# The first MLP product of a hybrid attention block in seven block products, and another order for the last output rows

## The chip, the cores and the metric

The kernel runs on one core of a Trainium2 chip. The metric is the time on the device in microseconds (us), as the median over runs. TensorE (PE, with its weight loads PEld) multiplies matrices, VectorE (DVE), ScalarE (ACT) and GpSimd (POOL) work elementwise, SyncE (SP) issues transfers. POOL and ACT can issue transfers as well. Each engine takes its own instructions in order and waits for the others on semaphores.

## The reference, cut to what matters

```python
h = x                                   # 512 rows x 1024
n = rmsnorm(h, g_mix); proj = n @ w_in  # two attention branches from here
h = h + merged @ w_out                  # merged: both branches, gated
m = rmsnorm(h, g_mlp)
h = h + jnp.square(jax.nn.relu(m @ w_ff1)) @ w_ff2    # w_ff1 1024 x 4096, w_ff2 4096 x 1024
return rmsnorm(h, g_final)
```

All in float32. The change lies in the first quarter of `m @ w_ff1` and in the last `rmsnorm`.

## The kernel before, in words

Every float32 matrix is split into a high part, rounded by ScalarE, and a low part, the difference, made by VectorE. A product is three matmuls (`mm3`, lines 88 to 90): high by high, and the two mixed ones. The two passes that make the parts are called the split of an operand; for a weight tile of 128 x 2 x 512 (1024 elements a partition) they are line 1616 (`hi`) and line 1620 (`lo`).

The MLP runs in four quarters of the 4096 hidden columns. In each quarter a first product (`f`, m by a 1024 x 1024 part of w_ff1) is followed by a second (`g`, its activated result by the matching part of w_ff2). Both factors are cut into 2 x 2 blocks. All the groups but the first, f0, use seven block products instead of eight: sums of the left blocks, sums of the right (weight) blocks, and sums of the results. For the left factor these sums are `m_sum` (line 1519, VectorE), split by `m_hi` and `m_lo` (lines 1508 and 1512); they are made once and serve all quarters. For the right factor `sum` adds blocks in place, by VectorE (line 1628) in the `f` groups and by a transfer issued by POOL that adds to what lies in the tile (line 1626) in the `g` groups. Each block product has 16 chunks (two column halves b, two row tiles i, four parts p of the contraction), each of three matmuls of 128 x 256: 48 matmuls. Weight block x lies in two tiles g (parts 0 and 1, and parts 2 and 3 of the contraction), and there are four such pairs: `wq` for B11, B12, B21 and `ring` for B22. `sink` takes a finished accumulator to where it goes: for f groups into the blocks `f..a..`, then relu, square, sums and splits for the second product.

f0 alone is `plain`: eight block products with the four weight blocks each used twice, B12, B11, B21 and B22 split two times, no weight sums. It starts right after the output projection (`wo_product`), while the residual rows 2 and 3 are still being finished: `add_rows` (line 1465) adds a finished part of the projection to the rows, `first_half_square` and `second_half_square` (line 174) give the sums of squares, `row_rstd` (VectorE line 181, POOL line 184) the reciprocal root, line 1847 the scaled rows, `flipped` (line 198) transposes them on TensorE, `m_copy` (ACT line 1503 or VectorE line 1501) takes the transposed blocks out of PSUM. Rows 0 and 1 come first and give column half 0 of m (blocks 1 and 2 of `m_raw`); rows 2 and 3 are transposed between the first and second block product and give blocks 4 and 0.

The order is written by hand: `step(at, what, ...)` puts each piece at a place on a line of time (100 units stand for about 1 us of TensorE), the steps are sorted by place, and `in_program_order` fixes that order on PE, ACT and DVE. For the quarters, `PLACES` holds the places; f0 has its own, `F0_RIGHT`. SP's and POOL's transfers are not in that fixed order: a scheduler places them, each behind the work that it has to wait for.

The last rows: for rows 0 and 1 the steps `out_first` (square of the right half, and the product of rows and final gain on POOL, line 1718), `out_square`, `out_left` (line 1729), `out_store`; for rows 2 and 3, `last_rows` runs the last block product in three pieces (one for rows 2, two halves for rows 3), adds them (line 1749), and then squares (line 1722), root (lines 1725, 181, 184), scaling (lines 1729, 1733) and store.

## Time and profile before

| what | value |
|---|---|
| median of 3 runs (lowest, highest) | 744.96 us (744.7, 745.11) |
| the profiled execution, and its span | 745.58 us, 743.9 us |
| TensorE busy, mean granted clock | 732.8 us, 0.995 |
| VectorE, ScalarE, GpSimd busy | 627.1, 493.3, 209.7 us |
| f0's first matmul, the second product's first | 412.09, 460.57 us |
| TensorE's last matmul, last store issued | 734.33, 739.89 us |

Times inside a run count from the start of the span. A timeline row has start, duration, engine, source line, operation, output tile, input tiles, shape, and in brackets how long the engine was idle before and what ended that. The duration of a row overlaps the next instruction on the engine by some 0.1 us, so the pitch (start to start) is what a queue costs. Buffer numbers are left out of tile names: `f030h` is f0, product 3, half 0, high part; `mh` and `ml` are the parts of m's blocks, `mb` the transposed banks, `w` and `w220f`, `w221f` the weight tiles, `h` the residual rows, `hp` their sums and roots, `ms` their scratch and output. A row of a stretch has its start and end, its length, busy time and count of PE, PEld, DVE, ACT and POOL, the granted clock, the busy share of the DMA engines and GB/s.

### The profile page before, as it was taken

The page shows a single profiled execution, that of the slowest core. Times are in us where ns is not written, and L with a number is a line of the kernel's source. Part 1 is how long each engine was busy: PE and PEld are TensorE (multiplying, and loading weights), DVE is VectorE, ACT ScalarE, POOL GpSimd, SP SyncE. Part 2 cuts the span into 40 slices and gives each one's busy share as a digit, 9 for nine tenths or more (in the row PEclk, how much of TensorE's full clock was granted, in tenths as well). Part 3 has the DMA queues.
Part 4 walks back from the last instruction along what each step waited for, and adds up shares of the span by engine and source line. Part 5 has one row for each costly group of instructions (what it writes and reads, how often), then busy time and mean ns, then how long its engine had stood idle before and what let it go on. Part 6 is the DMA issues. An engine that isn't in the chain of part 4 may idle for free.

```text
span 743.9 us, 11549 instructions
## 1 busy us (share of the span) xinstructions
PE 732.8 (99%) x4274; PEld 648.4 (87%) x4274; DVE 627.1 (84%) x863; ACT 493.3 (66%) x803; POOL 209.7 (28%) x276
## 2 busy tenths in 40 slices
PE   9999999999999999999999999999999999999995
PEld 7888888888888888898988999889988998899984
DVE  7777887889998787898898778998699869987896
ACT  7556575686596675888856778545774477537764
POOL 0732020242754633146751011100211012101215
PEclk9999999999999999999999999999999999999998
DMA  9849682521221334459887048761987087816763
GB/s 305 276 108 225 205 176 86 92 52 28 74 56 43 50 82 113 108 118 235 247 184 209 32 124 216 176 165 57 242 185 197 9 246 175 195 56 150 166 111 113
DMA packets 78344, 105.76 MB, mean 142 GB/s; under 512 B 15792, under 2 KB 34224, under 8 KB 78288
## 3 DMA queue, kind: packets, MB, share of 16 engines
q1 hardware_dynamic: 63088, 75.64, 32.8%
q0 software_dynamic: 14912, 29.10, 23.2%
q8 instruction: 33, 0.54, 0.3%
q10 hardware_dynamic: 288, 0.28, 0.1%
q14 instruction: 23, 0.19, 0.1%
HBM read 100.03 MB, written 2.10 MB: 137 GB/s over the span
## 4 chain that ended last, share of the span: by engine, by line
PE 93%; DVE 3%; issue 1%; ACT 1%; DMA 1%; POOL 0%; POOLq 0%; DVEq 0%; ACTq 0%
PE first L326 3%; PE tp L1122 2%; PE zb L88 1%; PE zb L89 1%; PE zb L90 1%; PE f3x L89 1%; PE f2x L90 1%; PE f3x L90 1%; PE f1x L90 1%; PE f1x L89 1%; PE f2x L89 1%; PE f2x L88 1%; PE f1x L88 1%; PE f3x L88 1%; PE av L89 1%; PE av L88 1%
## 5 line engine op out<-in xcount | busy, mean ns | idle before, releaser
L1626 POOL DMA_DIRECT2D w<-in_w_ff x32 | 38.6, 1205 | 262.3 <-DMA w<-in_w_ff 148.6
L1102 DVE TENSOR_REDUCE top<-s 128x1 f32<-128x512 f32 x32 | 21.6, 681 | 4.8 <-PE s L90 4.7
L1107 ACT ACTIVATE e<-s,top 128x512 f32<-128x512 f32 x32 | 22.0, 688 | 3.5 <-DVE top L1102 2.5
L94 DVE TENSOR_TENSOR pT<-tp,pT 128x512 fp32r<-128x512 f32 x32 | 21.8, 682 | 2.4 <-ACT pT L93 1.9
L93 ACT ACTIVATE pT<-tp 128x512 fp32r<-128x512 f32 x32 | 19.1, 596 | 3.2 <-PE tp L1122 3.2
L1122 PE MATMUL tp<-ident,e 128*128 128x128 f32 x128 | 19.4, 274 | 0.0
L88 PE MATMUL av<-pT,v 128*128 128x256 f32 x64 | 19.1, 299 | 0.0
L90 PE MATMUL av<-pT,v 128*128 128x256 f32 x64 | 18.2, 285 | 0.0
L89 PE MATMUL av<-pT,v 128*128 128x256 f32 x64 | 18.1, 283 | 0.0
L1122 PEld LDWEIGHTS tp<-ident,e 128*128 128x128 f32 x128 | 15.2, 140 | 3.2 <-ACT e L1113 0.7
L94 POOL TENSOR_TENSOR qF<-qk,qF 128x512 fp32r<-128x512 f32 x4 | 6.6, 1643 | 37.5 <-ACT qF L93 37.5
L667 POOL DMA_DIRECT2D gvw<-in_w_in x4 | 4.9, 1232 | 38.7 <-DVE gvw L672 34.0
L1628 DVE TENSOR_TENSOR w<-w,w 128x1024 f32<-128x1024 f32 x12 | 14.4, 1221 | 0.1
L667 POOL DMA_DIRECT2D zaw<-in_w_in x4 | 4.9, 1228 | 32.7 <-DVE zaw L672 28.0
L88 PE MATMUL s<-kbuf,q 96*128 96x512 f32 x32 | 14.1, 439 | 0.0
L980 POOL DMA_DIRECT2D w<-in_w_out x10 | 12.2, 1399 | 6.5 <-DVE bo60l L94 5.3
L1153 POOL TENSOR_TENSOR mx<-tb,yg 128x256 f32<-128x256 f32 x8 | 7.7, 964 | 19.7 <-DVE tb L1150 13.8
L577 ACT ACTIVATE bds<-bd 128x512 f32<-128x512 f32 x4 | 2.4, 598 | 15.8 <-PE bd L555 15.8
L89 PE MATMUL s<-kbuf,q 96*128 96x512 f32 x32 | 12.6, 395 | 0.0
L90 PE MATMUL s<-kbuf,q 96*128 96x512 f32 x32 | 12.6, 393 | 0.0
L1113 ACT ACTIVATE e<-e,tot 128x512 f32<-128x512 f32 x16 | 11.6, 726 | 1.3 <-DVE tot L1112 1.3
L89 PEld LDWEIGHTS av<-pT,v 128*128 128x128 f32 x64 | 12.2, 190 | 0.3
(2167 smaller groups left out, 3269.2 us busy)
## 6 DMA issues: line engine op xcount, KB each, us to landing
w<-in_w_ff SPq DMA_DIRECT2D x48, 512.0 KB, 5.2
w<-in_w_ff POOLq DMA_DIRECT2D x32, 512.0 KB, 6.3
w<-in_w_out POOLq DMA_DIRECT2D x10, 512.0 KB, 9.0
grw<-in_w_in SPq DMA_DIRECT2D x8, 512.0 KB, 8.5
zaw<-in_w_in SPq DMA_DIRECT2D x8, 512.0 KB, 7.2
gvw<-in_w_in SPq DMA_DIRECT2D x8, 512.0 KB, 4.6
w<-in_w_out SPq DMA_DIRECT2D x16, 256.0 KB, 5.7
w220f<-in_w_ff SPq DMA_DIRECT2D x8, 512.0 KB, 5.0
```

What stands on the lines that cost most here:

```text
L88: nc.tensor.matmul(acc, lh, rh, start=start, stop=False, skip_group_check=onto)
L89: nc.tensor.matmul(acc, lh, rl, start=False, stop=False, skip_group_check=onto)
L90: nc.tensor.matmul(acc, ll, rh, start=False, stop=stop, skip_group_check=onto)
L93: nc.scalar.activation(hi, src, AF.Copy)
L94: rest.tensor_tensor(lo, src, raw(hi), op=ALU.subtract)
L326: nc.tensor.matmul(f_accs[i], a[:, i * P : (i + 1) * P], b, start=k == 0 and x == 0, stop=k == KD - 1 and x == 2)
L980: nc.gpsimd.dma_start(d, rows.rearrange("(k t p) w -> p t k w", t=2, p=P)[:, x // 2], accum_op=ALU.add)
L1102: nc.vector.tensor_reduce(top, acc, axis=AX.X, op=ALU.max, negate=True)
L1107: nc.scalar.activation(e, acc, AF.Exp, bias=top, accum_out=tot[:, qt % 2 : qt % 2 + 1])
L1122: nc.tensor.transpose(tp[:, k * P : (k + 1) * P], e[:, k * P : (k + 1) * P], ident)
L1626: nc.gpsimd.dma_start(d, self.source(src, g), accum_op=ALU.add)
L1628: nc.vector.tensor_tensor(d, d, self.tiles(src)[g], op=ALU.add)
```

## The change

f0 takes the seven-product form of the other f groups, in the order 1, 2, 5, 6, 7, 4, 3, so `PLAIN` and its branches go. Its weight sums are made by adding transfers on POOL, as in the g groups: `sum(3)` adds B22 to the tile of B12 before f0 starts, `sum(1)` adds B12, `sum(2)` B22 and `sum(4)` B21 to the tile of B11, each after the split that uses the tile's content until then. The left block sums are needed one product after the transposes, so `m_sum` puts blocks 5 and 6 into tiles of their own, all eight copies are ScalarE's, and the places of f0's steps are new. The accumulators of product 5 and 3 lie in the other PSUM pool, and product 5's weight parts in another pool of tiles. f0's hidden blocks go through the same `relu`, `square` and sums as in the other quarters. The places of all later work start 386 units earlier (`FLIPS` 190 in the place of a slot of 576). Ahead of f0, both high parts of product 1 are made first and the second low part right after the row addition, and the low parts of block 2 go behind the last two row additions.

At the end, the final gain's tile is taken when it is loaded; square, root, right-half scaling and store are steps of their own, in another order; the two quarter squares of row 3 write two columns.

```diff
     def m_sum(m, b):
         into, x, y, op = {
-            5: (4, 0, 4, ALU.subtract), 7: (0, 1, 0, ALU.subtract), 6: (1, 5, 1, ALU.subtract), 3: (2, 2, 6, ALU.add),
+            5: (5, 0, 4, ALU.subtract), 7: (0, 1, 0, ALU.subtract), 6: (5, 5, 1, ALU.subtract), 3: (2, 2, 6, ALU.add),
         }[m]
+        if into not in m_raw:
+            m_raw[into] = pair_tiles(f"mr{into}")
...
-            self.order = tuple(self.PLAIN) if self.plain else (1, 2, 5, 3, 6, 7, 4) if self.second else (1, 2, 5, 6, 7, 4, 3)
+            self.order = (1, 2, 5, 3, 6, 7, 4) if self.second else (1, 2, 5, 6, 7, 4, 3)
...
         def hi(self, m, g):
-            self.right[m, g] = halves(2, S, f"{self.name}{m}{g}")
+            if (self.n, m) == (0, 5):
+                self.right[m, g] = [u4(f"{self.name}{m}{g}{x}") for x in "hl"]
+            else:
+                self.right[m, g] = halves(2, S, f"{self.name}{m}{g}")
...
             d = self.tiles(dst)[g]
-            if self.second:
+            if self.second or self.n == 0:
                 nc.gpsimd.dma_start(d, self.source(src, g), accum_op=ALU.add)
...
             if m in (1, 2, 5):
-                self.accs[m] = [ps("at" if m == 1 else "mm", f"{self.name}{'xwz'[m // 2]}{b}") for b in range(2)]
+                self.accs[m] = [ps("at" if (m == 5 if self.n == 0 else m == 1) else "mm", f"{self.name}{'xwz'[m // 2]}{b}") for b in range(2)]
...
+    def out_gains():
+        gfin = u4("gfin", F32, (P, D))
+        nc.gpsimd.dma_start(gfin, t["g_final"].partition_broadcast(P))
+        return gfin
...
+    def out_square(i, cols, n=1):
+        nc.scalar.activation(ms_rows[i][:, cols], hrow[i][:, cols], AF.Square, accum_out=hparts[i][:, n : n + 1])
+
+    def out_rstd(i, n=1):
         p = hparts[i]
+        nc.vector.scalar_tensor_tensor(
+            p[:, 3:4], p[:, n : n + 1], 1.0 / D, p[:, 2:3], op0=ALU.mult, op1=ALU.add
+        )
+        nc.gpsimd.tensor_tensor(p[:, 3:4], p[:, 3:4], mhalf, op=ALU.pow)
...
+    def out_right(i):
         o, rs = ms_rows[i], hparts[i][:, 3:4]
         nc.scalar.activation(o[:, S:D], o[:, S:D], AF.Copy, scale=rs)
...
+        last_part(0)
+        out_rstd(2)
+        out_square(3, cols[0])
+        last_part(1)
+        out_square(3, cols[1], 0)
+        out_right(2)
+        p = hparts[3]
+        nc.vector.scalar_tensor_tensor(p[:, 2:3], p[:, 1:2], 1.0 / D, p[:, 2:3], op0=ALU.mult, op1=ALU.add)
+        out_left(2)
         out_store(2)
+        out_rstd(3, 0)
         out_left(3)
+        out_right(3)
         out_store(3)
...
     phases[1].load(B11)
+    for g in range(2):
+        f0.sum(3, g)
     flipped(0)
-    f0.hi(1, 0)
+    for g in range(2):
+        f0.hi(1, g)
     f0.lo(1, 0)
+    f0.sum(1, 0)
...
     add_rows(3, 1, xs_[1], ALU.subtract)
+    f0.lo(1, 1)
+    f0.sum(1, 1)
...
     for b in range(2):
         m_hi(2, b)
-        m_lo(2, b)
     wo_product(4, (0,))
     add_rows(2, 0, xs_[0])
     wo_product(4, (1,))
     add_rows(3, 0, xs_[1])
+    for b in range(2):
+        m_lo(2, b)
...
+    step_pairs(0, {5: (930, 1100), 6: (1400, 1460), 7: (1990, 2050), 3: (2920, 2980)}, m_sum)
+    step_pairs(0, {5: (1060, 1115), 6: (1460, 1515), 7: (2055, 2110), 4: (2550, 2600), 3: (3345, 3400)}, m_hi)
+    step_pairs(0, {5: (1165, 1230), 6: (1540, 1600), 7: (2150, 2260), 4: (2610, 2670), 3: (3480, 3540)}, m_lo)
+    F0_PLACES = {
+        "F hi": {2: (340, 440), 5: (540, 640), 6: (1450, 1760), 7: (1985, 2090), 4: (2610, 2710), 3: (3140, 3240)},
+        "F lo": {2: (580, 690), 5: (810, 990), 6: (1640, 1870), 7: (2110, 2225), 4: (2730, 2845), 3: (3250, 3365)},
+        "F sum": {2: (930, 1110), 4: (1760, 1990)},
...
+        "G load": {B21: (1800, 1900), B12: (2240, 2350), B22: (3380, 3500)},
+    }
...
-        base, f, g = slot + q * PERIOD, phases[2 * q], phases[2 * q + 1]
+        base, f, g = FLIPS + q * PERIOD, phases[2 * q], phases[2 * q + 1]
...
-        step(base + (6950 if i < 2 else 7450) + i, out_first, i)
+        step(base + (7000, 7001, 7250, 7450)[i], out_first, i)
     for i in range(2):
-        step(base + 7240 + i, out_square, i, slice(0, S))
+        step(base + 7080 + i, out_square, i, slice(0, S))
+        step(base + 7180 + i, out_rstd, i)
         step(base + 7440 + 2 * i, out_left, i)
+        step(base + 7300 + i, out_right, i)
         step(base + 7441 + 2 * i, out_store, i)
```

More of the change, by code (lines that the diff above doesn't have):

```diff
@@ L1865, in step_product @@
                     at += SECOND * 3 if ph.second else FIRST
[L1867 to L1868 removed]
+    FLIPS = 190
     slot = 16 * FIRST
[L1870 to L1882 removed]
```

111 lines of the change are left out of this document (34 added, 77 removed), and 3 rows, old and new, of the table F0_PLACES.

## The prediction

> **What bounds the kernel now.** I read the page first (shares, clock, chain), then the granted work by stretches, then the timelines of each engine around the first MLP group and at the end.
>
> ```profile
> span 743.9 us, 11549 instructions
> PE 732.8 (99%) x4274; PEld 648.4 (87%) x4274; DVE 627.1 (84%) x863; ACT 493.3 (66%) x803; POOL 209.7 (28%) x276
> PE 93%; DVE 3%; issue 1%; ACT 1%; DMA 1%; POOL 0%; POOLq 0%; DVEq 0%; ACTq 0%
> 412.10:459.80 47.70, 47.47 (x395) 47.08 (x394) 39.91 (x53) 35.50 (x57) 5.85 (x6) 1.00 0.41 112
> ```
>
> TensorE is busy 99% and carries 93% of the chain that ended last; in the first MLP product (last row: PE, weight loads, DVE, ACT, POOL, clock, DMA) it idles 0.23 us of 47.7, at full clock. So a removed matmul is worth its pitch, as long as the operands arrive. VectorE, with 39.9 of 47.7, is next.
>
> ```profile
> 412.09 0.28 PE L88 MATMUL f0x<-mh,f010h 128*128 128x256 f32 x1
> 417.71 0.28 PE L90 MATMUL f0x<-mh,f011l 128*128 128x256 f32 x1
> 418.11 1.94 PE L198 MATMUL mb<-ident,ms 128*128 128x128 f32 x16
> 419.81 0.37 PE L88 MATMUL f0x<-mh,f020h 128*128 128x256 f32 x1
> 420.72 0.28 PE L89 MATMUL f0x<-ml,f021h 128*128 128x256 f32 x1
> 421.12 0.39 PE L90 MATMUL f0x<-mh,f021l 128*128 128x256 f32 x1
> 426.01 0.28 PE L88 MATMUL f0w<-mh,f030h 128*128 128x256 f32 x1
> 431.77 0.28 PE L88 MATMUL f0y<-mh,f040h 128*128 128x256 f32 x1
> 460.57 0.40 PE L88 MATMUL g0x<-g010h,f0h 128*128 128x512 f32 x1
> ```
>
> The rows show the eight block products (f030h is product 3, half 0, high part), transposes (mb) between the first and second, and the second MLP product from 460.57. One block product is 431.77 - 426.01 = 5.76 us: 48 matmuls at 0.12. From 412.09 to 426.01 are 13.92 us, two products are 11.52 and the transposes 1.70 (418.11 to 419.81): 0.70 of gaps. They stand at 417.71 to 418.11 (the scaled rows 2 and 3 came late) and 420.72 to 421.12 with its restart (the low half f021l came late); some 0.04 are the change of form at 419.81, which stays: 0.66.
>
> **The change, part by part.**
>
> *One product less.* The built program has 4170 matmuls instead of 4218. 48 x 0.12 = **-5.76 us**, all on the path, if the seven remaining products are fed.
>
> *The left operands.* Seven products need sums of blocks of m, made on VectorE; before, the second product was followed by one that needed nothing new. Now the third product (number 5) needs block 5 = block 0 - block 4 from the transposes just before. Prices:
>
> ```profile
> 416.80 1.05 ACT L1616 ACTIVATE f020h<-w 128x1024 fp32r<-128x1024 f32 x1
> 417.75 1.04 ACT L1616 ACTIVATE f021h<-w 128x1024 fp32r<-128x1024 f32 x1
> 407.38 1.22 DVE L1620 TENSOR_TENSOR f010l<-w,f010h 128x1024 fp32r<-128x1024 f32 x1
> 408.51 0.68 DVE L1465 TENSOR_TENSOR h<-h,wox 128x512 f32<-128x512 f32 x1
> 414.84 1.28 DVE L1465 TENSOR_TENSOR h<-h,wox 128x512 f32<-128x512 f32 x2
> 423.83 1.56 ACT L1503 ACTIVATE mr<-mb,gvec 128x256 f32<-128x256 f32 x4
> 425.78 1.17 ACT L1508 ACTIVATE mh<-mr 128x512 fp32r<-128x512 f32 x2
> 426.47 1.29 DVE L1512 TENSOR_TENSOR ml<-mr,mh 128x512 fp32r<-128x512 f32 x2 [0.47 <-ACT mh L1508]
> ```
>
> So a split half costs ACT 0.95 (pitch of the pair) and DVE 1.13 (407.38 to 408.51), a 512-wide one about 0.52 and 0.60 (each row's duration less 0.12 for the part that overlaps the next), four copies 1.42. I lay the new order of each engine out with these. VectorE follows 408.51 with f011l (409.1 to 410.35), the low halves of m1 (to 411.7) and then the two row additions, which stood at 414.84 behind f011l, m1 and m2; the low halves of m2 come after them. The scaled rows end at 417.0 and f021l at 419.4, ahead of the transposes (417.85) and of its use (420.3): both old gaps go, **-0.66**. ACT then runs f050h, f051h to 419.0, waits for the transposes (PE 417.85 to 419.9), copies until 422.7; DVE runs f050l to 420.5, block 5 half 0 from 421.4, f051l 422.05 to 423.3, half 1 to 423.9, the low halves to 425.2. Product 5 starts at 425.36 and reads half 1 after 0.72: met, by 0.9 us. That slack covers the eight copies; gone, each late us is a us of TensorE.
>
> *The right operands by adding transfers.* Before, all eight weight blocks came by plain loads. Now block 11 is one pair of tiles that goes round: split, add a block by a POOL transfer, split again, three times; each transfer waits for the last low half and the next split waits for its landing. These transfers exist later in the kernel:
>
> ```profile
> L1626 POOL DMA_DIRECT2D w<-in_w_ff x32: 1190/1204/1237, 438.8 to 718.2; - x32
> DMA to landing us min/median/max: 5.7/6.3/10.4
> w<-in_w_ff POOLq DMA_DIRECT2D x2, 512.0 KB, 9.7
> w<-in_w_ff POOLq DMA_DIRECT2D x1, 512.0 KB, 6.7
> 404.00:406.00 2.00, 2.00 (x15) 1.74 (x14) 1.38 (x2) 2.00 (x4) 0.00 (x0) 1.00 0.00 0
> ```
>
> (9.7: median of the pair issued at 438.8 and 440.6 beside SP's loads; 6.7: the issue at 458.9; the two before the last row are issues by POOL.) Eight transfers at 1.2 us of POOL, which has 5.9 us of work in 47.7: nothing there. What POOL queues behind them are the reciprocal roots of rows 2 and 3, at 415 in my order; the last transfer ahead of them is issued by 411.6. The pair for the seventh product goes first (403.4 on), into DMA engines that idle at 404 to 406 (last row). Call the landing time of the second half's first sum A, issued at 410.35 behind f011l; of its second sum B. If A is under 8.5, f051l is held by the copies, B is issued at 423.3, its split takes 1.05 + 1.22, and TensorE wants it at 432.05 (product 6 starts 431.1): the stall is about B - 6.5, not below 0.15 (DVE's own queue: two m6 low halves and f060l ahead). If A is over 9.6, it is A + B - 15.2. Ends: B = 5.7 gives 0.15; 9.7 and 9.7 gives 4.2. The first sums share the engines with two loads and two earlier sums, as the 9.7 row did; the second only with two loads, as the 6.7 row. A = 9.2, B = 6.8 lies between the two formulas, 0.3 to 0.8. I take **+0.7**. The third sum has 2.5 us to spare, the seventh product's tiles over 15.
>
> The Trainium skill, SBUF — State Buffer, "SBUF: two separate sides", warns that a POOL-issued transfer starves while VectorE holds the shared ports, and gives about 620 ns alone and 3100 overlapped. By it each sum would land some 2.5 us later and my total be about 742 (an estimate from that page); the 32 issue rows above, 1190 to 1237 beside a VectorE busy 84%, do not show it, and the same page exempts two-input additions, most of VectorE's work here.
>
> *VectorE's and ScalarE's load.* VectorE loses two right low halves (2.3) and four copies (1.4 at ACT's price, which now makes them), and gains six sinks of 512 columns (3.6): even, 39.9 against a stage of 42. ACT loses the same split's high halves (1.9), gains the copies (1.4) and six passes that apply the relu, which the sinks did themselves before (3.1): 35.5 becomes 38. Cover is thin, but no total exceeds 42, and the work that piles up (from product 7 on) is due 2 us or more after its place in my layout.
>
> *Moved loads on SP.* Block 21 of the second product is loaded when f020l is done, block 12 when f071l is; the stage uses them after 454. No cost. The final gain vector's tile is only allocated later; its transfer stands at the same place of POOL's queue.
>
> *The last rows.*
>
> ```profile
> 734.33 0.28 PE L90 MATMUL gend<-g341h,f3l 128*128 128x256 f32 x1
> 735.82 1.26 POOL L1718 TENSOR_TENSOR ms<-h,gfin 128x512 f32<-128x512 f32 x1
> 736.46 0.64 DVE L1725 SCALAR_TENSOR_TENSOR hp<-hp 128x1 f32<-128x1 f32 x1 [0.32 <-ACT ms L1722]
> 737.04 0.55 POOL L184 TENSOR_TENSOR hp<-hp,mhalf 128x1 f32<-128x1 f32 x1
> 737.13 0.42 ACT L1722 ACTIVATE ms<-h 128x256 f32<-128x256 f32 x1 [0.78 <-DVE hp L1725]
> 738.52 0.55 POOL L184 TENSOR_TENSOR hp<-hp,mhalf 128x1 f32<-128x1 f32 x1 [0.94 <-DVE hp L181]
> 739.11 0.75 DVE L1729 SCALAR_TENSOR_TENSOR ms<-h,hp,gfin 128x512 f32<-128x512 f32 x1 [0.66 <-POOL hp L184]
> 739.89 0.33 SPq L1734 DMA_DIRECT2D out<-ms  x1
> ```
>
> Row 2's root (737.04) waits behind POOL's product for row 3 (735.82 to 737.1), and the second quarter square (737.13) waits for VectorE to read the first's sum, because both write one column. Now the squares use two columns, and row 2's first half and POOL's product for row 2 come ahead of the scaling of rows 0 and 1. New order: last addition to 736.1 at the latest, quarter square and its sum 736.6, row 2 scaled 736.2 to 736.9, row 3's sum 737.0, root 737.6, scaling 738.4, store 738.4: **-1.5**. Bounds: 0 and -1.9 (no wait left but the sequence itself). The end of the run stays 4.0 us behind the last store.
>
> ```profile
> 726.51 1.30 POOL L1718 TENSOR_TENSOR ms<-h,gfin 128x512 f32<-128x512 f32 x1
> 727.22 1.68 DVE L1620 TENSOR_TENSOR g340l<-w,g340h 128x1024 fp32r<-128x1024 f32 x1
> 728.82 1.21 DVE L1620 TENSOR_TENSOR g341l<-w,g341h 128x1024 fp32r<-128x1024 f32 x1
> 729.03 2.16 POOL L1718 TENSOR_TENSOR ms<-h,gfin 128x512 f32<-128x512 f32 x1
> ```
>
> One move speaks against: the roots' sums of rows 0 and 1 now stand ahead of g341l. g340l took 1.68 because POOL's product had begun first; g341l won, and the product took 2.16. With the sums first, POOL's product may win: g341l ends at 731.4 instead of 730.0, TensorE stalls 1.0 at 730.45, and the last addition ends at 736.1 instead of 735.8. The sum above already uses 736.1.
>
> **Sum.** -5.76 - 0.66 + 0.7 - 1.5 = -7.2. The profiled execution took 745.58 (span 743.9, 1.7 around it) and would take 738.4; the median of the runs, 744.96, is 0.6 lower, so I predict **737.7**. A measurement tells 0.2%, 1.5 us.
>
> **Rivals.**
> *Late sums (741).* Both second-half sums land like the 9.7 row: stall 4.2, 744.96 - 7.92 + 4.2 = 741.2. For it: six transfers of 512 KB (four sums, two loads) are issued between 403 and 412. Against: 6.3 is the median of 32, and 6.7 with two loads beside it. VectorE keeping its waits (7.8 us in 47.7 before) in the shorter stage would give about the same. The Trainium skill, DMA: Bandwidth & Descriptors, "Issuing engines are not separate DMA queues", says that POOL's and SP's transfers share 16 engines and interleave; the 9.7 row agrees.
> *Slower (747.8).* The same two landings decide it: from A + B = 23.1 on, the stall eats the 7.92 gained.
>
> ```profile
> w<-in_w_out POOLq DMA_DIRECT2D x2, 512.0 KB, 11.4
> DMA to landing us min/median/max: 3.9/7.9/13.0
> ```
>
> 11.4 is the pair issued at 379.6 to 381 beside SP's loads, 13.0 the slowest landing of these tiles up to 450. Twice 13.0 is a stall of 10.8: 744.96 - 7.92 + 10.8 = 747.8. Against: those had five to six loads beside them, these two at most.
> *The tail gives nothing (739.2).* The 1.0 us stall at g341l and a root that still waits behind a product: 737.7 + 1.5.
> *No effect* would need the products to be paced by another engine; no row before shows that.
>
> **Numbers.** Forecast 0.70 (its own range 736.5 to 739.2), late sums 0.15, tail 0.09, slower 0.05, no effect 0.01. The range 736.4 to 741.2 takes in the forecast, the tail case and half of the late sums: some 0.83. Faster 0.94, same 0.01, slower 0.05.
>
> **What would show it.** The second product should start near 454.8 instead of 460.57; no gap at the transposes; a gap below 1 us at f060/f061; adding transfers landing in 6 to 10 us; the last store at 4.0 before the end and 1.5 us closer to TensorE's last matmul (5.6 us before). Wrong would be: a gap of several us at f05 or f06, a landing over 11, TensorE waiting in later products, or roots that still follow POOL's products.

## The result and the profile after

The changed kernel took 742.38 us (median of 7 runs, 740.22 to 743.55) against 744.96 for the kernel before (744.56 to 745.83): a ratio of 0.996, 95% interval 0.9945 to 0.9975. That is 2.6 us faster, where 7.2 were forecast; 742.38 lies above the range (736.4 to 741.2). The profiled execution took 743.55, with a span of 741.9.

First the page of the changed kernel (span, busy time of each engine, shares of the chain that ended last):

```profile
span 741.9 us, 11474 instructions
PE 728.0 (98%) x4226; PEld 643.0 (87%) x4226; DVE 626.1 (84%) x861; ACT 494.2 (67%) x809; POOL 219.4 (30%) x284
PE 84%; DVE 6%; DMA 4%; issue 3%; POOL 1%; ACT 1%; POOLq 0%; DVEq 0%; ACTq 0%
```

TensorE carried 93% of the chain before and 84% now; DVE and DMA have taken 6 and 4. Its timeline names the places (start, duration, instruction, and in brackets the wait before it with what ended it):

```profile
425.96 0.39 PE L89 MATMUL f0z<-ml,f050h 128*128 128x256 f32 x1 [0.30 <-DVE ml L1512]
432.85 0.38 PE L90 MATMUL f0x<-mh,f060l 128*128 128x256 f32 x1 [0.69 <-DVE f060l L1620]
434.58 0.39 PE L90 MATMUL f0x<-mh,f061l 128*128 128x256 f32 x1 [0.75 <-DVE f061l L1620]
447.18 0.36 PE L88 MATMUL f0x<-mh,f040h 128*128 128x256 f32 x1 [1.80 <-DVE f0a L1672]
458.77 0.40 PE L88 MATMUL g0x<-g010h,f0h 128*128 128x512 f32 x1
729.80 0.50 PE L89 MATMUL ge<-g341l,f3h 128*128 128x512 f32 x1 [0.85 <-DVE g341l L1620]
733.82 0.28 PE L90 MATMUL gend<-g341h,f3l 128*128 128x256 f32 x1
```

Against the pitch of the matmuls around them, TensorE lost 0.57, 0.95, 1.02 and 1.96 us at the first four rows, at products 5, 6, 6 and 4. So the second product starts at 458.77, 1.80 before the 460.57 of the kernel before; with the 4.5 us lost that is the 6.3 that the removed product and the two old gaps bring (6.42 forecast). At the end it lost 1.0 at g341l and 0.5 at g340l (0.3 at g340l in the kernel before).

The DMA engines, 400 to 450 us (queue: packets, MB, share of 16 engines; q0 is POOL's, q1 SP's):

```profile
q0 software_dynamic: 2403, 4.66, 56.1%
q1 hardware_dynamic: 2334, 4.48, 26.3%
```

The stretch rows give their mean busy share as the last but one number, 0.83 after and 0.37 before. The first row is the kernel before, the second the changed one:

```profile
400.00:450.00 50.00, 49.77 (x374) 47.32 (x373) 38.86 (x53) 37.91 (x64) 6.07 (x8) 1.00 0.37 100
```

```profile
400.00:450.00 50.00, 46.46 (x341) 43.56 (x341) 38.15 (x52) 38.67 (x68) 15.00 (x16) 1.00 0.83 184
```

56.1% of 50 us for 4.66 MB is 6.0 us of all 16 engines per MB, or 3.16 us for one 512 KB sum; a plain load takes 1.54 by the same sum. The prediction counted POOL's issue time and the time to landing, and never this time of the engines.

### The profile page after: what moved, and what is told of

Read it like the earlier page. It is cut to its first block, busy times and chain, and to the rows that moved or that the text cites. A ratio compares the mean times of both kernels' runs of the same rounds, so it can differ in the third digit from the quotient of the medians.

```text
span 741.9 us, 11474 instructions
## 1 busy us (share of the span) xinstructions
PE 728.0 (98%) x4226; PEld 643.0 (87%) x4226; DVE 626.1 (84%) x861; ACT 494.2 (67%) x809; POOL 219.4 (30%) x284
## 3 DMA queue, kind: packets, MB, share of 16 engines
q1 hardware_dynamic: 63088, 75.64, 32.5%
## 4 chain that ended last, share of the span: by engine, by line
PE 84%; DVE 6%; DMA 4%; issue 3%; POOL 1%; ACT 1%; POOLq 0%; DVEq 0%; ACTq 0%
DMA w<-in_w_ff 4%; PE first L326 3%; PE tp L1122 2%; PE zb L88 1%; PE zb L90 1%; PE zb L89 1%; DVE h L1465 1%; PE f1x L89 1%; PE f3x L90 1%; PE f1x L90 1%; PE f2x L90 1%; PE f2x L89 1%; PE f3x L89 1%; PE f3x L88 1%; PE f2x L88 1%
## 5 line engine op out<-in xcount | busy, mean ns | idle before, releaser
L1626 POOL DMA_DIRECT2D w<-in_w_ff x40 | 48.3, 1219 | 260.4 <-DMA w<-in_w_ff 137.1
L90 PE MATMUL av<-pT,v 128*128 128x256 f32 x64 | 18.2, 285 | 0.0
L1122 PEld LDWEIGHTS tp<-ident,e 128*128 128x128 f32 x128 | 15.2, 140 | 3.1 <-ACT e L1113 0.7
```

What stands on the lines that cost most here:

```text
L90: nc.tensor.matmul(acc, ll, rh, start=False, stop=stop, skip_group_check=onto)
L1122: nc.tensor.transpose(tp[:, k * P : (k + 1) * P], e[:, k * P : (k + 1) * P], ident)
L1626: nc.gpsimd.dma_start(d, self.source(src, g), accum_op=ALU.add)
```

## The experiments

All rows in one table: time, its spread, the ratio to the kernel before; and from each profile the start of the second product and the time from there to the last store's issue.

| kernel | median us (lowest to highest) | ratio, 95% interval | second product starts | from there to the last store |
|---|---|---|---|---|
| before | 744.96 (744.56 to 745.83) | | 460.57 | 279.32 |
| changed | 742.38 (740.22 to 743.55) | 0.996, 0.9945 to 0.9975 | 458.77 | 279.06 |
| changed, again | 743.10 (740.45 to 743.14) | 0.9964, 0.9952 to 0.9977 | 455.89 | 278.85 |
| without the sums | 738.59 (738.20 to 738.82) | 0.9913, 0.9899 to 0.9927 | 453.80 | 278.69 |
| sums as plain copies | 738.59 (738.22 to 739.60) | 0.9913, 0.9899 to 0.9926 | 453.95 | 278.55 |
| last rows alone | 744.62 (744.31 to 745.22) | 0.9996, 0.9987 to 1.0004 | 460.09 | 278.52 |
| pass 7 first | 741.43 (740.10 to 742.59) | 0.995, 0.9936 to 0.9963 | 457.57 | 278.65 |
| roots late | 742.20 (740.84 to 743.25) | 0.9961, 0.9949 to 0.9974 | 456.70 | 278.42 |
| six loads late | 745.66 (744.98 to 748.13) | 1.0011, 1.0002 to 1.002 | 455.80 | 283.78 |
| four loads late | 741.48 (740.63 to 742.01) | 0.9949, 0.9936 to 0.9963 | 456.80 | 279.38 |
| loads in the gaps | 744.84 (743.78 to 745.61) | 0.9992, 0.9983 to 1.0001 | 454.34 | 285.53 |
| block 11 in the gap | 745.77 (744.30 to 746.31) | 1.0004, 0.9995 to 1.0013 | 461.75 | 278.06 |
| one sum on VectorE | 741.64 (740.87 to 742.72) | 0.9952, 0.9938 to 0.9966 | 456.73 | 277.63 |
| products ahead of roots | 744.83 (743.36 to 746.18) | 0.9993, 0.9984 to 1.0002 | 458.63 | 279.92 |
| scalings in the waits | 741.86 (739.81 to 742.84) | 0.995, 0.9937 to 0.9964 | 455.64 | 277.66 |
| pass 7 first, scalings in the waits | 741.01 (740.59 to 742.58) | 0.9946, 0.9933 to 0.9958 | 456.51 | 277.67 |

### Are the stalls the sums'?

```diff
     def sum(self, x, g):
         d = self.tiles(dst)[g]
+        if self.n == 0 and x != 3:
+            return
```

> The changed kernel without the six adding transfers for the sums 1, 2 and 4 of the first MLP product (these additions are left out of the computation, so its weights are not the sums). Theory: TensorE's four new stalls in that product (0.57, 0.95, 1.02 and 1.96 us in the profile) all come from the landing of these transfers, the last by way of VectorE, whose pass over product 7 stands behind a low half that waits for the fourth sum. Then all four go, the second product's first matmul stands near 454.5 instead of 458.8, and the time is about 738.1, 4.3 us under the changed kernel's 742.4. Rival: VectorE and ScalarE pace the shorter stage themselves; then at least 2 of the 4.5 us stay and the time is 740 or more.

Measured 738.59. The second product's first matmul:

```profile
453.80 0.40 PE L88 MATMUL g0x<-g010h,f0h 128*128 128x512 f32 x1
```

No gap over 0.1 us is left in the first product. VectorE and ScalarE do the same work in the same order, so they don't pace the stage; the rival is out. The runs also lie within 0.6 us, where those of the changed kernel spread over 3.3.

### What is dear about them: the queue or the addition?

```diff
-                nc.gpsimd.dma_start(d, self.source(src, g), accum_op=ALU.add)
+                nc.gpsimd.dma_start(d, self.source(src, g))        # self.n == 0 only
```

> The changed kernel with the first product's adding transfers turned into plain copies of the same blocks from the same queue (the additions are left out of the computation). It measures the disputed cost by itself. In the changed kernel's trace, between 400 and 450 us, POOL's queue takes 56.1% of the engines for 4.66 MB and SP's takes 26.3% for 4.48 MB: 2.3 times as much per byte. Theory: the addition costs that; as copies the same transfers take about 28%, land in 4 to 6 us, and the stalls go: 738.4. Rival: POOL's queue itself is dear (its descriptors are written by software), whatever it carries; then the share stays near 56%, the landings near 8, and the time near 742.4.

Measured 738.59. From 439.99 on the second product's sums, which still add, lie on POOL's queue, so here are the DMA queues from 400 to 436 us, where it carries the copies alone:

```profile
q0 software_dynamic: 1117, 4.08, 34.8%
q1 hardware_dynamic: 1437, 2.77, 23.4%
```

and POOL's queue of the changed kernel in the same stretch:

```profile
q0 software_dynamic: 1665, 3.21, 53.7%
```

As copies the same transfers take 3.1 us of the engines per MB instead of 6.0 (1.61 for 512 KB instead of 3.16), land in a median of 5.1 us instead of 8.3, and every stall is gone; 0.4 to 0.5 us of the landing is POOL's shorter issue (0.72 to 0.80 instead of 1.20 us), the rest is on the engines. The addition costs twice the copy (the shares in the expectation give 2.05 per byte too, not 2.3). The rival is out: a copy from POOL's queue takes what SP's load takes in the same stretch, 3.1 against 3.0 us per MB.

### The four stalls, one by one

The sums go by the number in `sum`: the first, second and fourth are those made in block 11's tiles (the prediction calls the fourth the third), and `sum(3)` is block 12's. A landing is read from the start of the split that waits for it, less than 0.1 us behind it.

The fourth stall. The rows of the changed kernel's POOL, ScalarE and VectorE around it:

```profile
435.14 1.21 POOL L1626 DMA_DIRECT2D w<-in_w_ff  x1 [0.61 <-DVE mr L1521]
444.12 1.06 ACT L1616 ACTIVATE f041h<-w 128x1024 fp32r<-128x1024 f32 x1 [2.38 <-DMA w<-in_w_ff]
445.21 1.23 DVE L1620 TENSOR_TENSOR f041l<-w,f041h 128x1024 fp32r<-128x1024 f32 x1 [2.21 <-ACT f041h L1616]
446.35 0.68 DVE L1672 TENSOR_TENSOR f0a<-f0a,f0x 128x512 f32<-128x512 f32 x1
```

The second half of the fourth sum, issued at 435.14, landed at 444.1, 9.0 us later, beside the loads of block 12. VectorE waited for it in f041l, and behind f041l stood the pass over product 7 (f0a<-f0a,f0x) that empties the accumulator into which product 4 starts.

```diff
-            1: (1280, 1290), 2: (1310, 1745), 5: (1780, 1975), 6: (2300, 2555), 7: (2860, 3130),
+            1: (1280, 1290), 2: (1310, 1745), 5: (1780, 1975), 6: (2300, 2555), 7: (2840, 3130),
```

> The changed kernel with one step moved on VectorE: the pass over product 7's first half (which frees the accumulator that product 4 starts into) ahead of the low half f041l, which waits for the fourth sum's landing. Theory: the stall of 1.96 us at the start of product 4 shrinks to 0.3 (f041l itself is then needed some 0.3 before it is ready), the other three stay at 2.5 together, the time is 740.8. Rival: TensorE wanted f041l at the same moment anyway, the stall only moves by 0.7 us to a later matmul; 742.4.

Measured 741.43; the profile has no wait left at product 4, and the other three are there with 0.48, 1.01 and 0.91 (here and below at the late matmul alone; the first three numbers above hold another 0.1 each for the restart). The time moved by 1.0, not 1.6, and a second profile of the unchanged kernel shows why: this stall varies by itself.

> The changed kernel itself, beside the others on the same chip: 742.4. Its runs spread over 3.3 us where the kernel before spreads over 1.3 and the kernel without the sums over 0.6. Theory: the spread is that of the sums' landings, since VectorE and ScalarE wait for them; it stays 2 us or more here, and the two kernels with loads held back spread less. Rival: the spread was the chip's; all alike.

Measured 743.10, with a profiled execution of 740.45. Its rows for the same place:

```profile
434.28 1.20 POOL L1626 DMA_DIRECT2D w<-in_w_ff  x1 [1.42 <-DVE mr L1521]
440.88 1.06 ACT L1616 ACTIVATE f041h<-w 128x1024 fp32r<-128x1024 f32 x1
442.05 1.22 DVE L1620 TENSOR_TENSOR f041l<-w,f041h 128x1024 fp32r<-128x1024 f32 x1
455.89 0.40 PE L88 MATMUL g0x<-g010h,f0h 128*128 128x512 f32 x1
```

Here the fourth sum had landed within 6.6 us, f041h waited for nothing, and product 4 lost nothing. The two executions of one kernel differ by 3.1 us and the second product's start by 2.88; 0.62 of that stands ahead of the first product (its first matmul is at 412.13 and 411.51), so 2.3 are made in it. The loads of block 12 don't tell the two apart: they were issued at 436.89 and 438.62 in one and at 436.12 and 438.11 in the other. What differs is the distance to the sum's first half on POOL's queue:

```profile
433.33 1.20 POOL L1626 DMA_DIRECT2D w<-in_w_ff  x1 [6.88 <-DVE f060l L1620]
431.65 1.20 POOL L1626 DMA_DIRECT2D w<-in_w_ff  x1 [5.11 <-DMA w<-in_w_ff]
```

The first row is the first execution, where f060l was late: the halves follow each other by 1.81 us; in the second they follow by 2.63. In the other profiles the halves came 1.5 to 1.8 apart with these loads beside them and landed in 8.2 to 8.7, or 2.2 to 2.4 apart and landed in 6.8 to 7.5. So a late second sum seems to make the fourth one late; that was not tested by itself. With the fourth stall removed for good the runs still spread over 2.5, and 2.0 in a later variant, so the spread is not that stall's alone. Of the two kernels below with loads held back, which were to spread less, one does (four loads, 1.4) and one does not (six loads, 3.2).

The first three stalls come from the first two sums. The rows of POOL's issues and of the high parts on ScalarE that wait for their landing, in the changed kernel:

```profile
410.66 1.23 POOL L1626 DMA_DIRECT2D w<-in_w_ff  x1 [0.25 <-DVE f011l L1620]
420.98 1.24 POOL L1626 DMA_DIRECT2D w<-in_w_ff  x1 [4.49 <-DVE f050l L1620]
425.24 1.20 POOL L1626 DMA_DIRECT2D w<-in_w_ff  x1 [3.02 <-ACT mh L1508]
420.33 1.06 ACT L1616 ACTIVATE f051h<-w 128x1024 fp32r<-128x1024 f32 x1 [1.54 <-DMA w<-in_w_ff]
428.75 1.06 ACT L1616 ACTIVATE f060h<-w 128x1024 fp32r<-128x1024 f32 x1 [1.81 <-DMA w<-in_w_ff]
431.30 1.06 ACT L1616 ACTIVATE f061h<-w 128x1024 fp32r<-128x1024 f32 x1 [0.45 <-DMA w<-in_w_ff]
```

The first sum's second half took 9.7 us to land, the second sum's halves 7.8 and 6.1. To see what the loads beside them do, I held the loads of the second product back.

```diff
+                if self.n == 1 and x != B22:
...
+                            tc.add_manual_dep(
+                                ins, gates["loads"],
...
+            if (self.n, m, g) == (0, 4, 1):
+                gates["loads"] = nc.cur_bb.bb.instructions[at:][-1].name
...
-    phases[1].load(B11)
...
-        "G load": {B21: (1800, 1900), B12: (2240, 2350), B22: (3380, 3500)},
+        "G load": {B11: (2720, 2722), B21: (2724, 2726), B12: (2728, 2730), B22: (3380, 3500)},
```

> The changed kernel with SP's six loads of the second product's blocks 11, 21 and 12 held back until the fourth sum has landed (the high part f041h waits for it, and the loads wait for f041h); every other order stays. Theory: the sums land late because plain loads lie between them on the same 16 DMA engines, which are busy all the time from 405 to 431 us. Without them the six sums land in 5.7 to 7 us instead of 6 to 9.6, f051h comes 2 us earlier and with it the copies, the first three stalls (0.57, 0.95, 1.02) go to 0.5 together and the fourth (1.96) to 1.0 at most: the second product starts near 455.7 and the time is 739.4. Rival: a sum lands late by its own cost or because VectorE holds its descriptors up; then the landings stay over 7.5 and the time is 742.4. Second rival: the loads are now late for the second product, and TensorE waits behind 450; 743 or more.

In this kernel half of the second product's sum for block 12 is issued ahead of the load that it should be added to, so that part of its weights is not the sum. Measured 745.66: the theory held up to 455.80, as forecast, with 0.64 and 0.52 left of the stalls; then TensorE waited 1.19, 1.03, 1.29 and 1.03 from 466 on. POOL's row behind it:

```profile
455.05 3.69 POOL L1640 DMA_DIRECT2D w<-in_w_ff  x3 [18.20 <-DMA w<-in_w_ff]
```

POOL waited 18.2 us for block 12's load, and the second product's own first sums stood behind that transfer in its queue. The next kernel holds back four loads, those of blocks 11 and 21, and leaves block 12's at their places (2240, 2350).

> The changed kernel with only SP's four loads of the second product's blocks 11 and 21 held back until the fourth sum has landed; block 12's loads go ahead of them, so that POOL's queue does not stand behind them as it did when all six were held back (there POOL waited 18.2 us for block 12, and the two sums queued behind it came 3 us late for the second product). Theory: the first product's stalls shrink from 4.5 to about 1.5 as there (0.65 at f061l, 0.5 to 1.0 at product 4's start), the second product starts near 455.8 and this time keeps it: 739.4. Rival: the four loads, now issued from 441 on beside the second product's own sums, only move the late landing there; 741 or more.

Measured 741.48, the rival's value but not its reason: the second product lost only 0.3 us, and the time went into the fourth stall. Its rows:

```profile
418.21 1.08 ACT L1628 ACTIVATE f051h<-w 128x1024 fp32r<-128x1024 f32 x1
445.21 0.36 PE L88 MATMUL f0x<-mh,f040h 128*128 128x256 f32 x1 [1.64 <-DVE f0a L1686]
```

f051h waits for no landing any more (1.54 in the changed kernel) and starts 2.1 earlier, and two stalls are gone. The fourth is whole (1.80). Block 12's loads still lie beside the fourth sum, and its halves follow each other by 1.8 us; as this stall varies by itself from 0 to 1.96, one profile doesn't tell what made it.

### Order or volume?

> The changed kernel with the pass over product 7 ahead of f041l, and the second product's loads in the gaps between the sums: block 11 when f051h has run (the first sum has landed, the second is not issued), blocks 12 and 21 when f041h has run (the fourth sum has landed), and the second product's sum of block 12 that much later on POOL's queue. Theory (order): there is room for the loads between the sums; the six sums land without a load beside them, the stalls of the first product are 1 us or less, the second product starts at 455.2 or earlier, no wait over 0.5 us comes after it, and the time is 739.0 (742.7 less 3.7), with a spread under 1.5 us. Rival (volume): 16 engines are filled by sums and loads together until 475, whatever their order; then the stalls come back in the second product and the time is 741.0 or more.

```diff
+                                ins, gates[5 if x == B11 else 4],
...
-        "G load": {B21: (1800, 1900), B12: (2240, 2350), B22: (3380, 3500)},
+        "G load": {B11: (650, 652), B12: (2720, 2722), B21: (2724, 2726), B22: (3380, 3500)},
+        "G sum": {**PLACES["G sum"], 3: (2740, 2950)},
```

Measured 744.84. Rows of its TensorE and ScalarE, and one of its stretches (TensorE's granted clock is the third number from the end):

```profile
454.34 0.40 PE L88 MATMUL g0x<-g010h,f0h 128*128 128x512 f32 x1
464.15 1.06 ACT L1628 ACTIVATE g050h<-w 128x1024 fp32r<-128x1024 f32 x1 [4.66 <-DMA w<-in_w_ff]
469.28 0.68 PE L88 MATMUL g0z<-g051h,f0h 128*128 128x512 f32 x1 [1.32 <-ACT g051h L1628]
```

```profile
470.00:472.00 2.00, 1.46 (x4) 1.18 (x5) 2.00 (x4) 0.88 (x2) 1.20 (x1) 0.50 0.98 178
```

The first product is what I had forecast (454.34; the forecast said 454.8). But the loss came back some ten us later: the second product's sums landed late, TensorE waited 1.03, 1.49 and 1.03, and its clock fell to 0.50 for some 6.8 us on top. The rival is right in its outcome: what the gaps give the first product, the second one lacks.

> The same with the last rows' scalings in the waits of the additions. Theory (order): 1.2 less than without, 737.8, which is the time forecast for the change. Rival (volume): 739.8 or more.

Measured 744.67 (742.88 to 746.03): the same loss with the new end.

> The pass over product 7 ahead of f041l and the last rows' scalings in the waits, and of the loads only block 11's moved, to behind f051h (into the gap between the first and the second sum); blocks 12 and 21 stay where the change put them, so the second product loses nothing. Theory: the first stall (0.5 at product 5) goes and f061h comes 1.5 us earlier, so that the stalls at product 6 fall from 1.7 to 0.7; no wait over 0.5 us in the second product: 739.6. Rival (volume): what is won before 440 is lost behind it, 741 as without the move.

Measured 745.77; theory and rival both missed it. Rows of ScalarE and TensorE, and a stretch:

```profile
431.94 1.06 ACT L1628 ACTIVATE f060h<-w 128x1024 fp32r<-128x1024 f32 x1 [7.22 <-DMA w<-in_w_ff]
433.56 0.38 PE L88 MATMUL f0x<-mh,f060h 128*128 128x256 f32 x1 [2.73 <-ACT mh L1508]
```

```profile
436.00:440.00 4.00, 3.89 (x16) 3.60 (x17) 4.00 (x6) 4.00 (x8) 2.41 (x2) 0.50 0.39 46
```

The gap between the first and second sum already held block 21's two loads; with block 11's there are four, 4 x 1.54 = 6.2 us of all engines, issued from 418 on, just ahead of the second sum (420.5). It landed 11.4 us after its issue instead of 7.8, TensorE lost 2.89, 0.61 and 1.62 there, and the clock fell. Here the loads just ahead of the sum on the engines set its landing; nothing was free between the sums.

> The pass over product 7 ahead of f041l and the last rows' scalings in the waits, all loads where the change put them, and the sum for block 12 (blocks 12 + 22, issued first by POOL at 403) made by VectorE instead: two additions of 1.22 us in VectorE's waits behind f050l and ahead of f060l. Theory (volume): two adding transfers less ahead of the first sum are 6.3 us less of all 16 DMA engines (56.1% of 50 us for 4.66 MB, so 3.16 us for each of 512 KB); the first sums land in under 7.5 us, f050h and f051h no longer wait for them, the first stall (0.5) goes, those at product 6 fall from 1.7 to about 0.8, and nothing comes late behind 460: 739.5, with a spread of the runs under 1.5. Rival: VectorE, with 2.4 us more in a stage of 42, becomes what product 5 or 6 waits for: 741 or more.

```diff
-            if self.second or self.n == 0:
+            if self.second or (self.n == 0 and x != 3):
...
-    for g in range(2):
-        f0.sum(3, g)
...
-        "F sum": {2: (930, 1110), 4: (1760, 1990)},
+        "F sum": {2: (930, 1110), 4: (1760, 1990), 3: (815, 1470)},
```

Measured 741.64. The first stall went, as the theory had it, though the first sum's halves landed after 8.0 and 8.6 us and not under 7.5. Product 6 still lost 1.06 and 0.91: the second sum, beside block 21's loads, still took 7.4 us (421.05 to 428.45), and the time is no better than without the edit (741.01). So engine time saved ahead of the first sum did not reach the second one. Two additions less (6.3 us of the engines) brought the first sum's second half from 9.7 to 8.6 us; the four loads held back, of which two lay beside it (3.1 us), brought it to 6.7. As far as these runs show, what counts is what lies beside the transfer that is waited for, not the stage's total.

### The last rows

> The kernel before with the new order of the last rows alone. Theory from the changed kernel's trace: the last row's sequence gains some 1.5 us, but the low half g341l, behind POOL's product, holds TensorE up by 1.0 and the last half's high part by 0.2; the last store comes 0.3 us earlier at most and the time is 744.7, no difference that can be told. The prediction's own value for the tail, -1.5, would give 743.5. Rival: the tail's gain is whole and the first group gave less; then 743.5 or less.

Measured 744.62, a ratio of 0.9996 (0.9987 to 1.0004): no difference that can be told, as the theory had it. Its rows:

```profile
728.20 2.34 DVE L1620 TENSOR_TENSOR g341l<-w,g341h 128x1024 fp32r<-128x1024 f32 x1
738.61 0.38 ACTq L1746 DMA_DIRECT2D out<-ms  x1
```

And those of the changed kernel's end, which the experiments below take apart:

```profile
727.38 1.29 POOL L1716 TENSOR_TENSOR ms<-h,gfin 128x512 f32<-128x512 f32 x1
727.41 2.34 DVE L1620 TENSOR_TENSOR g341l<-w,g341h 128x1024 fp32r<-128x1024 f32 x1
730.87 2.44 DVE L1730 SCALAR_TENSOR_TENSOR ms<-h,hp,gfin 128x512 f32<-128x512 f32 x2
734.77 0.16 DVE L1723 SCALAR_TENSOR_TENSOR hp<-hp 128x1 f32<-128x1 f32 x1 [0.53 <-POOL ms L1716]
735.59 0.75 DVE L1730 SCALAR_TENSOR_TENSOR ms<-h,hp,gfin 128x512 f32<-128x512 f32 x1 [0.26 <-POOL hp L1726]
736.26 0.15 DVE L1723 SCALAR_TENSOR_TENSOR hp<-hp 128x1 f32<-128x1 f32 x1
737.83 0.38 ACTq L1739 DMA_DIRECT2D out<-ms  x1
```

POOL's product began 0.03 us before g341l, which took 2.34 instead of 1.21. The left scalings of rows 0 and 1 (2.44) stood ahead of the last additions, so row 2's square came late and its sum (734.77) held up the last addition behind it; row 3's sum (736.26) stood behind row 2's scaling, which waited for row 2's root, and that for row 2's sum.

```diff
-        step(base + 7180 + i, out_rstd, i)
+        step(base + 7232 + i, out_rstd, i)
```

> The changed kernel with the two small sums for the roots of rows 0 and 1 behind the low half g341l on VectorE, as they stood before. Theory: g341l then begins before POOL's product for row 1 and takes 1.2 us instead of 2.34, TensorE's stall of 1.0 us at g341l goes, its last matmul is 1.0 earlier; of that the last store keeps 0.5 to 1.0, since the roots come later and the scaling of rows 0 and 1 stands ahead of the last additions: 741.4 to 741.9. Rival: the scaling behind the late roots takes all of it; 742.4.

Measured 742.20, the rival's value. g341l took 1.21 and TensorE's 1.5 us at the end are gone, but the last store then came 5.0 us after the last matmul instead of 4.0: 0.4 to 0.6 is left of it in the profile (278.42 against 278.85 and 279.06).

```diff
-        step(base + (7000, 7001, 7250, 7450)[i], out_first, i)
+        step(base + (7000, 7001, 7178, 7350)[i], out_first, i)
...
-        step(base + 7180 + i, out_rstd, i)
-        step(base + 7440 + 2 * i, out_left, i)      # rows 0 and 1: into last_rows
+        step(base + 7232 + i, out_rstd, i)
...
```

> The changed kernel with the last rows in yet another order: the roots' sums of rows 0 and 1 behind g341l, the left scalings of rows 0 and 1 in the waits of the last rows' additions instead of ahead of them, POOL's products for rows 2 and 3 ahead of or between the roots, so that no root waits behind a product. Theory: the gain of 1.5 forecast for the last rows was there, but three waits hid it (g341l behind POOL's product, the last additions behind two scalings of 0.7 each, and row 2's root and then row 3's sum behind POOL's product for row 3). Without them TensorE's 1.5 us of stalls go and the last store follows TensorE's last matmul by 3.1 to 3.5 instead of 4.0: 2.0 to 2.4 less, 740.2. Rival: what can be had at the end is a few tenths; 741.5 or more.

Measured 744.83; the theory fell. VectorE's and ScalarE's issue rows:

```profile
733.73 0.92 DVE L1723 SCALAR_TENSOR_TENSOR hp<-hp 128x1 f32<-128x1 f32 x1 [2.38 <-ACT ms L1719]
738.30 0.36 ACTq L1739 DMA_DIRECT2D out<-ms  x1
```

With POOL's product for row 2 ahead of the roots of rows 0 and 1, ScalarE's scalings of those rows waited for the roots, row 2's square behind them on ScalarE, row 2's sum on VectorE 2.38 us for that, and the last addition behind the sum: ScalarE's store came 6.3 after the last matmul (732.04), SP's last one, at 738.55, 6.5. From the second product's start to the last store it is 0.8 to 1.1 longer than in the changed kernel's two profiles, and the span (743.4) ends 4.9 behind the last store where the changed kernel's ends 4.0 behind it: 1.7 to 1.9 together, of the 1.7 to 2.4 us by which the median is slower.

```diff
-        step(base + 7180 + i, out_rstd, i)
-        step(base + 7440 + 2 * i, out_left, i)
+        step(base + 7232 + i, out_rstd, i)
...
         last_part(0)
+        out_left(0)
...
         last_part(1)
...
+        out_left(1)
+        out_rstd(3, 0)
         out_left(2)
-        out_rstd(3, 0)
```

> The changed kernel with the roots' sums of rows 0 and 1 behind g341l and the two left scalings of rows 0 and 1 put into the waits of the last rows' additions, POOL's and ScalarE's order otherwise unchanged. (With POOL's products ahead of the roots, ScalarE's scalings of rows 0 and 1 waited for the roots and row 2's square behind them, and the last store came 6.3 us after TensorE's last matmul.) Theory: no stall of TensorE at g340l and g341l, the last addition 0.25 behind the last matmul's start instead of 1.0, row 3's sum no longer behind row 2's scaling: the last store follows the last matmul by 3.1 to 3.8, where the roots-late variant had 5.0. 740.4 to 741. Rival: ScalarE's and POOL's order sets the end; 742.

Measured 741.86. From the second product's start to the last store are 277.66 us, 1.2 to 1.4 less than in the changed kernel's two profiles and 1.7 less than before. But part of it comes back behind the store. ScalarE's last store and the span of this kernel:

```profile
733.30 0.38 ACTq L1739 DMA_DIRECT2D out<-ms  x1
span 738.1 us, 11475 instructions
```

The span ends 4.8 behind the last store, against the 4.0 that the prediction took as fixed and that the kernels before and changed have: the eight stores now leave within 4.0 us (from 729.32) instead of 6.9 (from 730.96). To the end of the span this stretch is 0.5 to 0.6 shorter than in the changed kernel and 0.9 shorter than before. So 0.9 of the 1.5 forecast for the last rows could be had by another order on VectorE. The store still follows the last matmul by 4.2: row 3's sum (731.30) stands behind row 1's scaling, and that behind a small sum which took 0.98 us beside POOL's product for row 3.

### Together

> The pass over product 7 ahead of f041l, SP's loads held back and the last rows in the new order, together. Theory: the stalls in the first product are 0.6 or less in place of 4.5 and the end is 2.2 shorter: 736.3, below the 737.7 forecast for the change. Rival: the held-back loads or the sums collide with later transfers; 738 or more.

Measured 748.55 (ratio 1.0043, 1.003 to 1.0055), with the same missing sum as the six loads held back. The first product lost 0.92, but the second waited 2.38, 1.03 and 1.12 from 465 on, and the clock fell to 0.50 from 470 to 476.

> The four held-back loads, the pass over product 7 ahead of f041l, and the last rows with the scalings in the waits, together. Theory: stalls of 1 us or less in the first product instead of 4.5 (-3.5), the end 1.4 to 2.0 shorter: 737.0 to 737.6. Rival: as for the two parts; 739 or more.

Measured 741.91 (ratio 0.9956, 0.9944 to 0.9969): the second product started at 455.01, and 2.4 us of new waits lay in it, the longest 0.97 at g051l.

> The pass over product 7 ahead of f041l and the last rows' scalings in the waits, with the loads where the change put them. Theory: the fourth stall, which the landing of the fourth sum made 0 to 1.96 in the profiles so far (1.0 in the mean), goes, the three others (1.9 to 2.6 together) stay, the end is 1.2 shorter: 740.5, and the spread of the runs is 1.5 or less instead of 3, if it was that stall that spread them. Rival: the spread stays at 3; then it comes from the first two sums or from elsewhere.

Measured 741.01 (740.59 to 742.58), the lowest median of all kernels that compute the whole. It beats the kernel before by 4.0 us (ratio 0.9946, 0.9933 to 0.9958) and the changed kernel by 1.4 in the median; these two intervals overlap, so the second is likely and not shown.

## Why the prediction was wrong

- *One product less, -5.76, and two old gaps, -0.66.* Right. With the sums left out or made copies the second product starts at 453.80 and 453.95, 6.6 to 6.8 before the 460.57 of the kernel before; counted from f0's first matmul (411.76, 411.92 and 412.09) it is 42.04 and 42.03 against 48.48, so 6.4 less.
- *Left operands, "met, by 0.9 us".* Wrong: the first sum's landing held f051h (1.54), the eight copies behind it on ScalarE, and with them the low half ml that product 5 reads, so the 0.9 of slack was used up and 0.57 lost.
- *The stall, +0.7.* The step that failed most: 0.7 was forecast, and the changed kernel's profile has 4.5. The two landings in the formula came as estimated: A was 9.7 (410.66 to 420.33; estimate 9.2), B 6.1 (425.24 to 431.30; estimate 6.8), and A + B - 15.2 gives 0.6. But the formula priced only the second halves' first two sums. The first half's second sum landed after 7.8 and, through the splits that stood behind f060h on ScalarE and VectorE, put f060l late (0.95); the first landing also pushed B's issue from the 423.3 of my layout to 425.24 (1.02 at f061l); and the fourth sum cost up to 1.96. The landings were long because each sum held the 16 engines for 3.16 us, twice a load, which the prediction did not count: as copies they cost no stall at all.
- *"The third sum has 2.5 us to spare", and "the work that piles up is due 2 us or more after its place".* Wrong for that sum (the fourth above) and for the pass over product 7 behind it: I looked at when f041l itself was due, not at what stood behind f041l on VectorE.
- *Size over all runs.* The mean of the changed kernel's 12 runs is 742.26, 2.8 below 745.10, the mean of the runs of before on the same two occasions; with -6.42 and the -0.6 below, the stalls come to some 4.2 (an estimate from these means); the kernel without the sums, 738.59, lies 3.7 below the same mean. That is the size of the late-sums rival, by another way than the one I gave it.
- *The last rows, -1.5.* Wrong by 0.9: the six profiles with this end and an undisturbed second product lie 0.3 to 0.8 under the kernel before (mean 0.6). "Last addition to 736.1 at the latest" failed, as the additions stood behind the scalings of rows 0 and 1 beside POOL's product, and row 3's sum stood behind row 2's scaling: on the clock of the kernel before, 1.80 later, the last addition ended at 737.07 and row 3's sum began at 738.06, where 737.0 was forecast. The stall at g341l came as forecast, 1.0; it wasn't absorbed, and g340l lost 0.2 more than before.
- *The numbers.* Late sums and a tail that gives nothing were two rivals with chances of 0.15 and 0.09, each worked out as if the other stayed away. Both came, though neither whole (stalls of 3.7 to 4.2, and a tail that gave 0.6): 737.7 + 3.5 + 1.5 is 742.7, and 742.38 was measured. The range reached to one of them only.
- *The rule that POOL's transfers starve behind VectorE.* The Trainium skill, SBUF — State Buffer, "SBUF: two separate sides", would have given 742 by the prediction's estimate, near the result, but by luck and not by its way: in the changed kernel 39 of POOL's 40 issues took 1.19 to 1.24 us (one 1.68), and the landings fell from 8.3 to 5.1 when the same transfers only copied, with VectorE busier (36.5 us of the 42 from 412 to 454, against 32.5).

## What to carry to other kernels

A transfer that adds has two prices, the issue and the time that it takes from all 16 engines; the second stands in the profile as share over MB by queue (in a stretch where the queue carries one kind of transfer only), and it belongs in the sum for every transfer beside it. When a wait is judged by its slack, look at what is queued behind the waiting instruction on its engine, since that decides who stalls. Here two small failures of one plan came together; a range should hold their sum, not only each.

## What the runs showed of the hardware

- An adding transfer of 512 KB took 3.16 us of all 16 DMA engines, the same bytes copied from the same queue 1.61, loaded from SP's 1.54 to 1.59. The Trainium skill, Collectives: The Full Stack, "The bandwidth ceiling: the fold count and why AG ≠ RS ≠ AR", puts it down to the two source reads of the addition that a ReduceScatter gets half the bandwidth of an AllGather. Here, outside a collective, 6.0 against 3.1 us per MB is the same factor.
- Two profiled executions of the same kernel differed by 3.1 us, and 2.3 of it lay in the stage with such transfers (one of them landed 6.6 or 9.0 us after its issue). Without the additions four runs each lay within 0.6 and 1.4, those of the kernel before within 1.3.
- TensorE's clock fell to 0.50 near 469.4 (its mean is 0.86 from 468 to 470), after waits of 1.03 and 1.49 us within 4 (loads in the gaps), and near 435.1 (0.78 from 434 to 436), after 2.89 and 0.61 within 5 (block 11 in the gap), for some 6.8 us each time; it stayed at 1.00 after a single wait of 1.96, and after 1.19, 1.03, 1.29 and 1.03 within 7. The Trainium skill, TensorE: Matmul & The Clock Gate, "What's actually happening", lets the clock halve after an idle window of about 3.4 us that runs freely: the halving agrees, but no wait here lasted 3.4. What decides between these cases stays open.
